# RWKV stage of a one-core decoder step: TensorE's order written out in 137 slots, weight granules fetched two ahead

## The chip, the core and the metric

One core of one Trainium2 chip runs the whole program in one launch. The metric is the device time of that launch in microseconds (us). Five engines work side by side, each through its own queue in order: TensorE (PE, matmuls; its weight loads are shown apart as PEld), VectorE (DVE), ScalarE (ACT), GpSimd (POOL) and SyncE (SP), which here only issues DMAs. They wait for one another by semaphores.

## What is computed

One layer of a recurrent decoder for 320 tokens: a prompt of 256 and 8 samples of 8 new tokens each. A wide projection feeds three branches (HGRN2, RWKV-7, a short gated convolution); they are merged through gates, and an output mix and an MLP follow. The part that the change touches is the RWKV branch and the convolution beside it. Cut to what matters:

```python
rw = proj[..., OFF_RW:OFF_SC]                       # 26 column tiles of 128
xs = rw + (prev - rw) * rw_mu                       # token shift
r, kr, vr, wd, ad, gd = jnp.split(xs, cuts, axis=-1)
decay = exp(-exp(-softplus(-(rw_w0 + tanh(wd) @ rw_w2)) - 0.5)); a = sigmoid(rw_a0 + ad @ rw_a2)
kk = normalized(kr * rw_k_k); k = kr * (1 + (a - 1) * rw_k_a)
# per token: S = S*w + (S @ -kk) (kk*a) + v k ;  o = S r
o_rw, rw_S = _rwkv7_scan(r_, w_, k_, v_, kk, a_, rw_S0)
o_rw = (groupnorm(o_rw) * rw_ln_w + rw_ln_b + bonus) * (sigmoid(gd) @ rw_g2)
y_b = o_rw @ w_pb
u = sc * sh; y_c = (sb * conv3(u)) @ w_pc           # short convolution branch
```

## The kernel before

All activations lie transposed, 128 channels by 320 tokens. A weight matrix is cut into granules of 128 x 1024 floats (512 KB), eight blocks of 128 x 128 for one column tile. `granule` loads one into `raw`, and `split` makes two halves of it on the fly: ACT casts it to `whi_t` (L104) and DVE subtracts to get `wlo_t` (L105), in two pieces of 512 columns. `dense` multiplies 16 blocks (two granules) into one PSUM tile `mm_t`, three matmuls a block (L130 to L132), 48 for a tile. The three buffers each of `raw`, `whi_t` and `wlo_t` are all the lookahead there is.

After a short prologue (norm, the first two column tiles) the RWKV stage works through 8 units of two heads each (`j`). A unit needs three projected tiles (k, r, v, through `shift_mix`), then a chain of small fp32 matmuls with DVE, ACT and POOL work between them:

- `rwkv_front` (L371 to L459): decay and gates, normalised keys, the tiles LYR, BK, X, BT; two reciprocals on DVE (L166, L400).
- `rwkv_solve` (L461 to L549): products of them (L481), a 16 x 16 triangular inverse on DVE in 30 short steps (L512, L514) with a trip through DRAM before and after, and two levels of block inversion on TensorE (L537, L541, L547).
- `rwkv_chunks` (L551 to L679): four chunks of the prompt one behind the other. A chunk is three exchanges: L581/L582, ACT copies Y (L584), L589, DVE copies X (L591), L593/L594, DVE makes the next state (L599 or L601). Behind them in the same function the samples (L614 to L634), the group norm (L642 to L663) and the output (L673 to L679), which is written to `self.B` in SBUF.

`short_conv` projects three more tiles (SC, SH, SB) a unit and leaves its result in `self.Cb` in SBUF. The loop at L360 to L367 writes, for each unit, the solve of the next, the chunks of this one, one convolution, and the front of the one after. The framework's scheduler then orders every engine's queue by priority (the order in which the code was traced) and by its own estimates of time, TensorE's too. Thereafter `merge_split` splits `Cb` into `bh`/`bl`, and HGRN2, the merges with `w_pc`, `w_pb` (from `B`) and `w_pa`, the output mix and the MLP follow; the change leaves their code alone, except that `merge_split` for two of the three sources loads from DRAM.

Of the kernel before, what the change touches and what calls it, by code (L numbers as in the profile page):

```python
# [83 lines left out]
SC_ORDER = ((), (0,), (1,), (2,), (3,), (4,), (5,), (6, 7))  # L84


class K:
# [32 lines left out]
    def dense(self, granules, ah, al):  # L120

        ps = self.mm.tile([128, 512], F32, name="mm_t")
        n = len(granules) * 8
        i = 0
        for g in granules:
            hi, lo = self.granule(g)
            for k in range(8):
                w = slice(k * 128, k * 128 + 128)
                mmul = self.nc.tensor.matmul
                mmul(ps[:, :NT], hi[:, w], ah[:, i, :], start=(i == 0), stop=False)  # L130
                mmul(ps[:, :NT], hi[:, w], al[:, i, :], start=False, stop=False)  # L131
                mmul(ps[:, :NT], lo[:, w], ah[:, i, :], start=False, stop=(i == n - 1))  # L132
                i += 1
        return ps[:, :NT]

# [17 lines left out]
    def proj(self, n):  # L153
# [3 lines left out]
        return self.dense([w[n, 0], w[n, 1]], self.xh, self.xl)  # L157

# [15 lines left out]
    def build(self):  # L174
# [94 lines left out]
        self.merge_split(self.Cb)  # L269
# [5 lines left out]
        for src, i, w in ((self.B, 1, io["w_pb"]), (self.A, 0, io["w_pa"])):  # L275
            self.merge_split(src)
# [14 lines left out]
    def shift_mix(self, wp, n, name, packed):  # L291

        nc = self.nc
        ps = self.proj(n)
# [12 lines left out]
        xs = wp.tile([128, NT], F32, name="xs" + name, bufs=2 if name == "v" else 1)  # L307
# [7 lines left out]
    def rwkv(self, cx):  # L315
# [21 lines left out]
        for nm, cols in (("Nb", 640), ("GB0", 640), ("GB1", 640), ("LX", 256), ("Ms", 256), ("Od", 640)):  # L337
# [21 lines left out]
        st.append(self.rwkv_front(1, wp, w2))
# [9 lines left out]
        nc.sync.dma_start(io["o_shift"], self.shl)  # L369

    def rwkv_front(self, j, wp, w2):  # L371
# [5 lines left out]
        kx = self.shift_mix(w2, RK + j, "k", False)  # L377
        r = self.shift_mix(w2, RR + j, "r", False)
        vx = self.shift_mix(w2, RV + j, "v", True)
# [17 lines left out]
        W = w2.tile([128, NT], F32, name="W")  # L397
        V.tensor_mul(W, Wp, wt[:, 1:])
        Wi = wp.tile([128, NT], F32, name="Wi")
        V.reciprocal(Wi, W)  # L400


        sq = wp.tile([128, NT], F32, name="sq")
# [8 lines left out]
        LYR = w2.tile([128, 5, 4, 64], F32, name="LYR")  # L412
        BK = w2.tile([128, 5, 3, 64], F32, name="BK")
# [12 lines left out]
        S.copy(BK[:, :, 2, :], BK[:, :, 0, :])  # L426
        rk = wp.tile([128, NT], F32, name="rkk")
        V.scalar_tensor_tensor(rk, r, self.par("rk", j), t, ALU.mult, ALU.mult)


        X = w2.tile([128, 5, 2, 64], F32, name="X")
# [12 lines left out]

        bs = self.pa.tile([128, 512], F32, name="pa_t")
# [12 lines left out]

        return W, LYR, BK, X, BT, vx  # L459

    def rwkv_solve(self, j, front, wp):  # L461
        nc, io = self.nc, self.io
        V, G, S, T = nc.vector, nc.gpsimd, nc.scalar, nc.tensor
        W, LYR, BK, X, BT, vx = front
# [5 lines left out]
        Nb = Z["Nb"].rearrange("p (c w) -> p c w", w=128)  # L470
        GB = Z["GB%d" % (j % 2)].rearrange("p (c h w) -> p c h w", h=2, w=64)
        for mk, cc in (("mkp", slice(0, 4)), ("mks", slice(4, 5))):
# [10 lines left out]
            for h, rows in ((0, lo), (1, hi)):  # L483
# [10 lines left out]
                if n == 1:  # L494
                    V.tensor_mul(GB[orow, cc, h, :], p3[orow, :n, cr], mc(orow, cr))

# [6 lines left out]
        nc.sync.dma_start(flat(dN), Z["Nb"])  # L503
# [11 lines left out]
        for c in range(5):  # L515
            nc.sync.dma_start(blocks(dP, c), Pd[8 * c:8 * c + 8])
        nc.sync.dma_start(Z["Pm%d" % (j % 2)], flat(dP))
# [15 lines left out]
        for h in (16, 32):  # L533
            T3 = Z["T%d" % h].rearrange("p (c w) -> p c w", w=128)
            ps = self.pinv.tile([128, 512], F32, name="pi")
            for i in range(4):
                T.transpose(ps[:, blk(i)], Pm[:, i, :], ident)  # L537
            S.copy(Z["Mm"], ps)
            ps = self.pinv.tile([128, 512], F32, name="pi")
# [4 lines left out]
            V.tensor_mul(lev4(Z["T%d" % h], h, 0), ps[:, 0:256].rearrange("p (c n w) -> p c n w", c=4, w=h), mb)  # L544
            ps = self.pinv.tile([128, 512], F32, name="pi")
# [5 lines left out]
    def rwkv_chunks(self, j, front, wp, w2):  # L551
        nc, io = self.nc, self.io
        V, G, S, T = nc.vector, nc.gpsimd, nc.scalar, nc.tensor
        W, LYR, BK, X, BT, vx = front
        Z = self.Z
        ident = self.cst("id")
        lo, hi = slice(0, 64), slice(64, 128)
        GB = Z["GB%d" % (j % 2)].rearrange("p (c h w) -> p c h w", h=2, w=64)
        Pm = Z["Pm%d" % (j % 2)].rearrange("p (c w) -> p c w", w=128)
        s0 = wp.tile([128, 8, 64], F32, name="s0")  # L560
        nc.sync.dma_start(s0, io["s_rw"][j])
        lg = wp.tile([128, 128], F32, name="lg")
        nc.sync.dma_start(lg, io["lg"][:, j * 128:j * 128 + 128])
# [6 lines left out]
        flat = lambda t: t.rearrange("p h w -> p (h w)")  # L570
        alpha = lambda c: flat(LYR[:, c, 0:2, :])
        rho = lambda c: flat(LYR[:, c, 2:4, :])
# [4 lines left out]
        otm = wp.tile([128, 5, 64], F32, name="otm")  # L577
        for c in range(4):
            wc = W[:, c * 64 + 63:c * 64 + 64]
# [5 lines left out]
            if c:  # L585
                for h, rows in heads:
                    G.tensor_scalar_mul(Sw[rows, :], X[rows, c, h, :], wc[rows])
            up = self.py.tile([128, 512], F32, name="py_t")
            T.matmul(up[:, 0:64], Pm[:, c, :], Y, start=True, stop=True)  # L589
            for h, rows in heads:  # L590
                V.tensor_copy(X[rows, c, h, :], up[rows, 0:64])  # L591
            sp = self.py.tile([128, 512], F32, name="py_t")
# [9 lines left out]
        nc.sync.dma_start(io["o_rwp"][j], sn)  # L602
        for h, rows in heads:
            S.copy(otm[rows, 0:4, :], ot4[rows, :, hb(h)])

        LX = Z["LX"].rearrange("p (b a h t) -> p b a h t", a=2, h=2, t=8)
# [12 lines left out]
        yp = self.py.tile([128, 512], F32, name="py_t")  # L621
# [4 lines left out]
        up = self.py.tile([128, 512], F32, name="py_t")  # L626
# [3 lines left out]
        os = self.py.tile([128, 512], F32, name="py_t")  # L630
# [33 lines left out]


        o = wp.tile([128, 5, 64], F32, name="o")
        vx3 = vx.rearrange("p (c w) -> p c w", w=64)
        for cc in (slice(0, 4), slice(4, 5)):
# [5 lines left out]
            for h, rows in heads:  # L674
                V.scalar_tensor_tensor(o[rows, cc], t3[rows, 0:n, hb(h)], self.par("lnw", j)[rows], vx3[rows, cc],
                                       ALU.mult, ALU.add)
        gp = self.pa.tile([128, 512], F32, name="pa_t")
        T.matmul(gp[:, :NT], lg, self.Lg, start=True, stop=True)
        V.tensor_mul(self.B[:, j, :], gp[:, :NT], o.rearrange("p c w -> p (c w)"))  # L679
# [30 lines left out]
    def short_conv(self, j):  # L710
# [4 lines left out]
        scp = self.proj(SC + j)  # L715
        sc = wp.tile([128, NT], F32, name="sc")
        V.tensor_mul(sc, scp, self.rs)
        shp = self.proj(SH + j)
# [14 lines left out]
        sbp = self.proj(SB + j)  # L733
# [466 lines left out]
```

## Time and profile before

| | us |
|---|---|
| median of 3 runs | 2466.48 (2465.77 to 2467.6) |
| the profiled execution's own time | 2465.12 |
| its span in the profile | 2463.3 |
| PE busy, share of the span | 98% |
| PEld busy | 94% |
| DVE, ACT, POOL busy | 61%, 40%, 14% |
| RWKV stage in the trace (end of the prologue's norm to the last write of `B`) | 28.8 to 567.0 |

A row of the windows view gives, for a stretch, its length and then busy time and number of instructions of PE, PEld, DVE, ACT and POOL, the granted clock, the share of DMA time and GB/s. In rows of the lines view stand busy time, mean duration of one in ns, and the idle time of the engine just before it with what ended it. A matmul's end is modelled, so neighbouring rows overlap: the distance between starts is what a matmul costs, not its duration.

### The profile page before, as it was taken

What the parts mean: (1) busy time and instruction counts of PE and PEld (TensorE: products, weight loads), DVE (VectorE), ACT (ScalarE), POOL (GpSimd) and SP (SyncE); (2) the same over time, 40 slices, a digit from 0 to 9 for tenths busy, and PEclk for the clock granted to TensorE, in tenths of its full rate; (3) what the DMA queues carried; (4) which work ended last, traced back from release to release, by engine and by line L of the source; (5) the groups of instructions that cost most, each with busy time, mean ns of one, the idle gap of its engine ahead of it and who ended that gap; (6) DMA issues with size and microseconds to landing.
All of it is one profiled execution on the core that took longest, in us unless ns stands there. A gap on an engine that the chain in (4) does not pass through costs nothing.

```text
span 2463.3 us, 41900 instructions
## 1 busy us (share of the span) xinstructions
PE 2420.1 (98%) x16246; PEld 2325.6 (94%) x16246; DVE 1504.2 (61%) x3097; ACT 996.8 (40%) x1937; POOL 355.8 (14%) x508
## 2 busy tenths in 40 slices
PE   8999999999999999999999999999999999999998
PEld 7888898889999999999999897999999999999996
DVE  6788888866566656655555446754555555555555
ACT  6444444434444344433343435344333333333333
POOL 4333332220000111011111331200000000000003
PEclk9999999999999999999999999999999999999999
DMA  5433333334433333344444654444444444444443
GB/s 192 131 96 122 104 122 107 121 125 142 138 132 138 133 134 128 124 155 152 147 152 146 238 184 165 154 151 148 153 148 152 147 153 149 151 147 153 148 152 129
DMA packets 132278, 354.93 MB, mean 144 GB/s; under 512 B 34928, under 2 KB 43504, under 8 KB 132080
## 3 DMA queue, kind: packets, MB, share of 16 engines
q1 hardware_dynamic: 132080, 352.25, 41.5%
q8 instruction: 129, 2.11, 0.3%
q14 instruction: 69, 0.57, 0.1%
HBM read 337.06 MB, written 15.14 MB: 143 GB/s over the span
## 4 chain that ended last, share of the span: by engine, by line
PE 90%; DVE 6%; POOL 1%; issue 1%; ACT 1%; DMA 0%; SPq 0%; DVEq 0%; ACTq 0%; POOLq 0%
PE mm_t L132 26%; PE mm_t L130 26%; PE mm_t L131 26%; DVE wlo_t L105 1%; PE pi L481 1%; PE pho_t L874 1%; PE pi L541 1%; PE plv_t L834 1%; PE plv_t L835 1%; DVE t L512 0%; PE pi L547 0%; PE py_t L581 0%; DVE Pd L514 0%; DVE rn_y L166 0%; DVE Wi L400 0%
## 5 line engine op out<-in xcount | busy, mean ns | idle before, releaser
L104 ACT CAST whi_t<-raw 128x512 fp32r<-128x512 f32 x1192 | 685.8, 618 | 1161.1 <-PE mm_t L131 728.8
L105 DVE TENSOR_TENSOR wlo_t<-raw,whi_t 128x512 fp32r<-128x512 f32 x1192 | 828.5, 725 | 311.3 <-ACT whi_t L104 300.1
L130 PE MATMUL mm_t<-xh,whi_t 128*128 128x320 f32 x2048 | 643.8, 314 | 1.2 <-DVE Rk L301 1.2
L132 PE MATMUL mm_t<-xh,wlo_t 128*128 128x320 f32 x2048 | 641.8, 314 | 0.4 <-DVE wlo_t L105 0.4
L131 PE MATMUL mm_t<-xl,whi_t 128*128 128x320 f32 x2048 | 640.5, 313 | 0.0
L130 PEld LDWEIGHTS mm_t<-xh,whi_t 128*128 128x128 f32 x2048 | 386.2, 189 | 4.9 <-ACT xsv L448 1.5
L132 PEld LDWEIGHTS mm_t<-xh,wlo_t 128*128 128x128 f32 x2048 | 386.0, 189 | 3.3 <-issue 0.9
L131 PEld LDWEIGHTS mm_t<-xl,whi_t 128*128 128x128 f32 x2048 | 386.0, 188 | 2.0 <-issue 0.2
L130 PE MATMUL mm_t<-hh,whi_t 128*128 128x320 f32 x1232 | 381.4, 310 | 0.0
L131 PE MATMUL mm_t<-hl,whi_t 128*128 128x320 f32 x1232 | 380.7, 309 | 0.0
L132 PE MATMUL mm_t<-hh,wlo_t 128*128 128x320 f32 x1232 | 380.6, 309 | 0.0
L132 PE MATMUL mm_t<-rh,wlo_t 128*128 128x320 f32 x1024 | 316.4, 309 | 0.0
L130 PE MATMUL mm_t<-rh,whi_t 128*128 128x320 f32 x1024 | 316.4, 309 | 0.0
L131 PE MATMUL mm_t<-rl,whi_t 128*128 128x320 f32 x1024 | 316.4, 309 | 0.0
L130 PEld LDWEIGHTS mm_t<-hh,whi_t 128*128 128x128 f32 x1232 | 231.5, 188 | 6.5 <-ACT sqt L1031 4.9
L131 PEld LDWEIGHTS mm_t<-hl,whi_t 128*128 128x128 f32 x1232 | 231.5, 188 | 0.0
L132 PEld LDWEIGHTS mm_t<-hh,wlo_t 128*128 128x128 f32 x1232 | 231.4, 188 | 0.0
L130 PEld LDWEIGHTS mm_t<-rh,whi_t 128*128 128x128 f32 x1024 | 192.2, 188 | 0.0
L131 PEld LDWEIGHTS mm_t<-rl,whi_t 128*128 128x128 f32 x1024 | 192.2, 188 | 0.0
L132 PEld LDWEIGHTS mm_t<-rh,wlo_t 128*128 128x128 f32 x1024 | 192.2, 188 | 0.0
L1102 DVE TENSOR_TENSOR m<-m,mm_t 128x320 f32<-128x320 f32 x112 | 54.6, 488 | 189.5 <-PE mm_t L132 189.5
L1032 POOL TENSOR_TENSOR ssf<-ssf,sqt 128x320 f32<-128x320 f32 x14 | 14.1, 1005 | 841.5 <-issue 809.3
(424 smaller groups left out, 2733.3 us busy)
## 6 DMA issues: line engine op xcount, KB each, us to landing
raw<-w_in SPq DMA_DIRECT2D x256, 512.0 KB
raw<-w_ff SPq DMA_DIRECT2D x256, 512.0 KB
raw<-w_o SPq DMA_DIRECT2D x32, 512.0 KB
hs<-s_hg SPq DMA_DIRECT2D x16, 512.0 KB
raw<-w_pc SPq DMA_DIRECT2D x16, 512.0 KB
raw<-w_pb SPq DMA_DIRECT2D x16, 512.0 KB
raw<-w_pa SPq DMA_DIRECT2D x16, 512.0 KB
o_hgs<-hsn SPq DMA_DIRECT2D x16, 256.0 KB
```

Of the source, the lines that this page charges most:

```text
L104: self.nc.scalar.copy(hi, src)
L105: self.nc.vector.tensor_sub(lo, src, hi)
L130: mmul(ps[:, :NT], hi[:, w], ah[:, i, :], start=(i == 0), stop=False)
L131: mmul(ps[:, :NT], hi[:, w], al[:, i, :], start=False, stop=False)
L132: mmul(ps[:, :NT], lo[:, w], ah[:, i, :], start=False, stop=(i == n - 1))
L481: T.matmul(pp[h][:, i, :], BK[rows, c, h:h + 2, :].rearrange("p a w -> p (a w)"), LYR[rows, c, h:4:2, :], start=True, stop=True)
L541: T.matmul(ps[:, half(i)], Nb[:, i, :], cols(Mm[:, i, :], h, 0), start=True, stop=True)
L834: T.matmul(ps[:, 0:64], KS[:, 0:128], rh[:, 0:hb], start=True, stop=True)
L835: T.matmul(ps[:, 64:128], KS[:, 128:256], rh[:, hb:2 * hb], start=True, stop=True)
L874: T.matmul(op[:, 256:320], s0[:, b, :], QX[:, 64 * b:64 * b + 64], start=(b == 0), stop=False)
L1032: (nc.vector if last else nc.gpsimd).tensor_add(acc, acc, t)
L1102: nc.vector.tensor_add(d, d, ps)
```

## The change

The three functions of a unit become generators that stop at their hand-overs, and so does `dense`, after each block of three matmuls. The group norm and output become `rwkv_tail`, the samples `rwkv_sample`. One loop over 137 slots then writes TensorE's order (`manual_schedule` for PE alone): in slot t, each of the 8 units takes the steps that the tables put there (a unit starts 12 slots after the one before), and then dense blocks are written, 7 a slot in the first 12 slots and 5.5 a slot afterwards. Other engines and the DMA queue are still ordered by the scheduler. Steps of `chunk` and `sample`, the late steps of `solve`, and every fetch of a granule are traced at a priority of 1000 ahead. `fetch` keeps three granules requested: the one in use and two ahead. Convolution tiles are spread: eight of 24 in between the units' tiles, sixteen behind them. `B` and `Cb` no longer lie in SBUF: each 128 x 320 piece is stored to DRAM (`dB`, `dC`) and loaded again, through two buffers `bsrc`, when it is split. Buffers change: `W` and `xsv` 4 (from 2), `LYR`, `X`, `BT`, `GB` 3 (from 2), `Nb` 2 (from 1), `otm` 2 (from 1), `BK` 1 (from 2).

```diff
-SC_ORDER = ((), (0,), (1,), (2,), (3,), (4,), (5,), (6, 7))
+NSLOT = 12
+URGENT = 1000
+FRONT = (-6, -5, 0, 1, 2)
+SOLVE = (1, 2, 9, 15, 16, 17, 18, 19, 20)
+SAMPLE = (20, 21, 22, 23)
+CONV = (3, 0, 1, 1, 1, 1, 1, 0)
+CHUNK = tuple(range(21, 33))
+TAIL = (33, 39, 40)
...
+    def fetch(self):
+        while len(self.ahead) < 3 and self.order:
+            n, h = self.order.pop(0)
+            with self.tc.high_priority(offset=URGENT):
+                self.ahead.append(self.granule(self.io["w_in"][n, h]))
+        return self.ahead.pop(0)
...
-        for j in range(8):
-            if j < 7:
-                self.rwkv_solve(j + 1, st[j + 1], wp)
-            self.rwkv_chunks(j, st[j], wp, w2)
-            for i in SC_ORDER[j]:
-                self.short_conv(i)
-            if j < 6:
-                st.append(self.rwkv_front(j + 2, wp, w2))
+        blocks = (50 - len(self.early)) * 16
+        chains = ((front, FRONT), (sample, SAMPLE), (chunk, CHUNK), (solve, SOLVE), (tail, TAIL))
+        total = 8 * NSLOT + TAIL[-1] + 1
+        with self.tc.manual_schedule(engines={mybir.EngineType.PE}):
+            done = 0
+            for t in range(total):
+                for j in range(8):
+                    for chain, slots in chains:
+                        if t - NSLOT * (j + 1) in slots:
+                            if chain in (chunk, sample) or slots is SOLVE and t - NSLOT * (j + 1) > 9:
+                                with self.tc.high_priority(offset=URGENT):
+                                    next(chain[j], None)
+                            else:
+                                next(chain[j], None)
+                while done < max(7 * min(t + 1, NSLOT), blocks - (blocks - 7 * NSLOT) * (total - 1 - t) // (total - NSLOT)):
+                    next(dense, None)
+                    done += 1
...
-        V.tensor_mul(self.B[:, j, :], gp[:, :NT], o.rearrange("p c w -> p (c w)"))
+        of = o.rearrange("p c w -> p (c w)")
+        V.tensor_mul(of, gp[:, :NT], of)
+        nc.sync.dma_start(self.dB[j], of)
...
-    def merge_split(self, src):
+    def merge_split(self, src, wp):
         for k in range(8):
-            self.split(self.bh[:, k, :], self.bl[:, k, :], src[:, k, :])
+            if wp is None:
+                t = src[:, k, :]
+            else:
+                t = wp.tile([128, NT], F32, name="bsrc")
+                self.nc.sync.dma_start(t, src[k])
+            self.split(self.bh[:, k, :], self.bl[:, k, :], t)
```

TensorE before, two exchanges of one chunk in the middle of the stage (unit 2; L581, L589 and L593 are the chunk's matmuls, the others dense):

```order
L581 MATMUL py_t<-X,LYR 128x128
L582 MATMUL po_t<-X,LYR 128x128
L131 MATMUL mm_t<-xl,whi_t 128x320
L132 MATMUL mm_t<-xh,wlo_t 128x320
L589 MATMUL py_t<-Y,Pm_388 128x64
L130 MATMUL mm_t<-xh,whi_t 128x320
L131 MATMUL mm_t<-xl,whi_t 128x320
L132 MATMUL mm_t<-xh,wlo_t 128x320
L130 MATMUL mm_t<-xh,whi_t 128x320
L131 MATMUL mm_t<-xl,whi_t 128x320
L593 MATMUL py_t<-X,BT 128x128
```

TensorE of the change, an exchange of the same kind (L685 is the old L589, L690 the old L593, L740 and L745 belong to the samples of the same unit, L142 to L144 are the dense matmuls):

```order
L740 MATMUL pa_t<-Y_2430,Pm_400 128x64
L685 MATMUL py_t<-Y,Pm_400 128x64
L142 MATMUL mm_t<-xh,whi_t 128x320
L143 MATMUL mm_t<-xl,whi_t 128x320
L144 MATMUL mm_t<-xh,wlo_t 128x320
...
L745 MATMUL pa_t<-c,Ms 128x128
L746 MATMUL pa_t<-X,GB_408 128x128
L690 MATMUL py_t<-X,BT 128x128
```

Before, two to five dense matmuls stand between a chunk's matmul and the one that needs its result back; now 15 (as here) or 18 do, in every slot.

DVE before, from the copies of X (L591) to the state (L601) of a first chunk, unit 1:

```order
L591 COPY X<-py_t 64x64 x2
L619 COPY Ms<-pa_t 64x4x4x8 x2
L601 TENSOR_SCALAR X<-py_t,W 64x64 x2
L300 TENSOR_TENSOR Rk<-mm_t,rs 128x256
```

DVE of the change at the same place (L687 is the old L591, L698 the old L601, L116 the split of a granule):

```order
L687 COPY X<-py_t 64x64
L602 TENSOR_TENSOR t_2140<-Nd,Pd 40x3x13
L116 TENSOR_TENSOR wlo_t<-raw,whi_t 128x512 x2
...
L772 TENSOR_TENSOR otm<-otm,gs 128x320
L861 SCALAR_TENSOR_TENSOR cv<-u,p,cv 128x336
L776 TENSOR_REDUCE gv<-sq_2475 128x5
L698 TENSOR_SCALAR X<-py_t,W 64x64 x2
```

Twenty-five instructions now stand between the copies and the state at this place, where two stood; a similar stretch stands in unit 0, and in the later units a few instructions do.

SP before, where the merge with `w_pb` begins, issues weights alone:

```order
L112 DMA raw<-w_pb 128x1024
L112 DMA raw<-w_in 128x1024 x2
L112 DMA raw<-w_pb 128x1024
L112 DMA raw<-w_in 128x1024 x2
L112 DMA raw<-w_pb 128x1024
```

SP of the change at the same place (`bsrc<-dB` are the pieces of the RWKV output; the first two of the eight were loaded long before):

```order
L123 DMA raw<-w_pb 128x1024
L123 DMA raw<-w_in 128x1024 x2
L1095 DMA bsrc<-dB_348 128x320
L1095 DMA bsrc<-dB_349 128x320
L123 DMA raw<-w_pb 128x1024
L1095 DMA bsrc<-dB_350 128x320
L1095 DMA bsrc<-dB_351 128x320
L123 DMA raw<-w_in 128x1024
L1095 DMA bsrc<-dB_352 128x320
L1095 DMA bsrc<-dB_353 128x320
```

Six loads, each pair of which needs the two buffers that the splits of the pair before give back, now stand in this queue among the weights.

More of the change, by code (lines that the diff above doesn't have):

```diff
@@ L125, in dense @@
         for g in granules:
-            hi, lo = self.granule(g)
+            hi, lo = self.fetch() if g is None else self.granule(g)
             for k in range(8):
@@ L133, in dense, with run @@
                 i += 1
+                if i < n:
+                    yield
         return ps[:, :NT]
+    @staticmethod
+    def run(steps):
+        while True:
+            try:
+                next(steps)
+            except StopIteration as e:
+                return e.value
+    def dense(self, granules, ah, al):
+        return self.run(self.dense_steps(granules, ah, al))
     def dense_wide(self, tiles, ah, al, psp, wpool):
@@ new lines, in rwkv @@
+        dense = self.rwkv_dense(w2)
+        front = [self.rwkv_front(j, wp, w2) for j in range(8)]
+        solve = [self.rwkv_solve(j, wp) for j in range(8)]
+        chunk = [self.rwkv_chunks(j, wp, w2) for j in range(8)]
+        sample = [self.rwkv_sample(j, wp) for j in range(8)]
+        tail = [self.rwkv_tail(j, wp) for j in range(8)]
+        blocks = (50 - len(self.early)) * 16
+        chains = ((front, FRONT), (sample, SAMPLE), (chunk, CHUNK), (solve, SOLVE), (tail, TAIL))
+        total = 8 * NSLOT + TAIL[-1] + 1
@@ new lines, in rwkv @@
+        with self.tc.manual_schedule(engines={mybir.EngineType.PE}):
[12 more added lines that the diff above has]
+                    done += 1
+            self.run(dense)
+            for c in front + solve + chunk + sample + tail:
+                assert next(c, 0) == 0
@@ L368, in rwkv, with rwkv_dense @@
         nc.sync.dma_start(io["o_cv"], self.cvo)
         nc.sync.dma_start(io["o_shift"], self.shl)
+    def rwkv_dense(self, w2):
+        S = self.nc.scalar
+        tiles, conv = [], [(c, j) for j in range(8) for c in (SC, SH, SB)]
+        for j in range(8):
+            tiles += [(RK, j), (RR, j), (RV, j)] + ([(RG, 0)] if j == 1 else [])
+            for _ in range(CONV[j]):
+                tiles.append(conv.pop(0))
+        tiles = [(RWA, 0)] + tiles + conv
+        self.order = [(n + j, h) for n, j in tiles if n + j not in self.early for h in range(2)]
+        self.ahead = []
+        done = {}
+        for n, j in tiles:
+            if n in (SC, SH, SB):
+                c = done.setdefault(j, self.short_conv(j))
+                for end in c:
+                    yield
+                    if end:
+                        break
+                continue
+            name = {RK: "k", RR: "r", RV: "v", RWA: "k", RG: "k"}[n]
+            quick = n + j in self.early
+            xs = yield from self.shift_mix(w2, n + j, name)
+            if n == RWA:
+                S.activation(self.L[0:64, :], xs[0:64, :], AF.Tanh)
+                S.copy(self.L[64:128, :], xs[64:128, :])
+            elif n == RG:
+                S.activation(self.Lg, xs, AF.Sigmoid)
+            else:
+                self.st[j][name] = xs
+            if not quick:
+                yield
```

158 lines of the change are left out of this document (101 added, 57 removed).

## The prediction

> **What bounds the kernel now.** The views in the order in which I read them: the windows view, to find where TensorE loses time; the timeline at one hand-over, to see what a loss looks like; the lines view of DVE, for what its queue holds. Windows first: the RWKV stage, then a piece of its beginning, four units of its middle, and three stretches after it.
>
> ```profile
> 28.80:567.00 538.20, 515.02 (x3467) 467.78 (x3466) 435.03 (x1149) 236.21 (x499) 168.30 (x334) 0.99 0.35 116
> 28.80:160.00 131.20, 120.30 (x767) 108.30 (x766) 103.45 (x267) 61.05 (x120) 48.34 (x109) 0.96 0.37 121
> 224.00:289.00 65.00, 62.99 (x432) 56.89 (x432) 53.35 (x147) 28.61 (x63) 23.49 (x42) 1.00 0.33 110
> 289.00:354.00 65.00, 63.03 (x434) 57.57 (x433) 52.16 (x140) 28.85 (x61) 19.73 (x38) 1.00 0.36 118
> 354.00:419.00 65.00, 63.25 (x434) 58.03 (x434) 53.75 (x142) 29.16 (x62) 20.26 (x40) 1.00 0.36 117
> 419.00:484.00 65.00, 63.23 (x435) 58.12 (x434) 53.70 (x143) 29.36 (x62) 18.14 (x33) 1.00 0.37 119
> 616.00:677.00 61.00, 61.00 (x422) 59.34 (x421) 36.20 (x82) 24.34 (x48) 5.34 (x6) 1.00 0.41 138
> 1170.00:1231.00 61.00, 61.00 (x418) 61.00 (x418) 35.13 (x55) 24.55 (x48) 7.70 (x6) 1.00 0.42 147
> ```
>
> From 616 us on PE has no idle time, and in dense work (1170 to 1231) PEld has none either: nothing is to be had there. In the RWKV stage PE is idle for 538.2 - 515.0 = 23.2 us, nearly half of it (10.9) before 160 us, and PEld for 538.2 - 467.8 = 70.4 us. What has to be known is how much of that is waiting. One hand-over in the middle, PE's rows and then ACT's:
>
> ```profile
> 301.45 0.46 PE L581 MATMUL py_t<-X,LYR 128*128 128x128 f32 x2
> 301.75 0.39 PE L582 MATMUL po_t<-X,LYR 128*128 128x128 f32 x2
> 301.89 0.39 PE L132 MATMUL mm_t<-xh,wlo_t 128*128 128x320 f32 x1
> 302.12 0.31 PE L130 MATMUL mm_t<-xh,whi_t 128*128 128x320 f32 x1
> 302.79 0.43 PE L589 MATMUL py_t<-Y,Pm 128*128 128x64 f32 x2 [0.36 <-ACT Y L584]
> 301.70 0.58 ACT L730 ACTIVATE cv<-u,p 128x336 f32<-128x336 f32 x1 [1.93 <-POOL u L726]
> 302.30 0.44 ACT L584 COPY Y<-py_t 64x64 f32<-64x64 f32 x2
> ```
>
> Two dense matmuls are all the cover between L581 and L589; ACT is busy with L730 until 302.28, copies Y after it, and PE stands. A dense matmul costs 61.00 / 418 = 0.146 us from the 1170 row, but 0.67 us pass between the starts at 302.12 and 302.79: 0.52 is lost, and the row shows 0.36. So PE's 23.2 us are too little, because the modelled end of a matmul covers the first part of a wait. PEld's 70.4 are too much, because a small fp32 matmul keeps the weight path less busy than a dense one. I take the middle, **46.8 us**, and keep both ends. A page bears on this choice: the Trainium skill, Perfetto Trace Analysis, section Identifying the Most-Contended Engine, says to judge TensorE by the busy share of its weight loads and not by that of its matmuls. By the page alone the loss would be 70.4; the 1170 row agrees in dense work, and the hand-over lies between the two.
>
> **The change, part by part.** First the PE floor of the stage. It holds 48 tiles of 48 dense matmuls:
>
> ```profile
> L130 PE MATMUL mm_t<-xh,whi_t 128*128 128x320 f32 x766 | 246.2, 321 | 1.2 <-DVE Rk L301 1.2
> ```
>
> 766 of the 768 of this line are in the trace; 3 x 768 x 0.146 = 336.4 us. The other 201.8 us are small matmuls and waits; less 46.8 this leaves 155.0, or 19.4 us of small matmuls a unit. The change removes and adds none of either. It only puts 15 or 18 dense matmuls, 2.2 or 2.6 us, behind every step, where two to five stood; the exchange above takes about a microsecond when nothing is in its way (0.46 for L581, 0.44 for the copies, and the hops). **Term 1: -46.8 us** (from -23.2 to -70.4) if every hand-over is covered.
>
> Second, what stays late. PE's time falls and DVE's does not, so DVE is what to look at:
>
> ```profile
> L105 DVE TENSOR_TENSOR wlo_t<-raw,whi_t 128x512 fp32r<-128x512 f32 x191 | 128.9, 693 | 11.4 <-ACT whi_t L104 9.0 <-ACT Y L584 1.1
> L166 DVE RECIPROCAL rn_y<-rn_t 128x320 f32<-128x320 f32 x8 | 17.1, 2136 | 0.0
> L400 DVE RECIPROCAL Wi<-W 128x320 f32<-128x320 f32 x8 | 16.9, 2114 | 0.0
> L731 DVE SCALAR_TENSOR_TENSOR cv<-u,p,cv 128x336 f32<-128x336 f32 x8 | 4.5, 567 | 2.6 <-ACT cv L730 2.5
> L717 DVE TENSOR_TENSOR sc<-mm_t,rs 128x320 f32<-128x320 f32 x8 | 3.9, 490 | 1.2 <-PE mm_t L132 1.0
> ```
>
> In the four middle units DVE is busy 53.2 us of 65, with six tiles (12 granules) each. In the change a unit comes every 12 slots. 768 dense blocks less the 84 of the first 12 slots, over 125 slots, are 5.47 a slot; 12 slots hold 65.7 blocks, or 8.2 granules, 65.7 x 3 x 0.146 = 28.8 us of PE, and with 19.4 a period of **48.2 us**. DVE has 3.8 granules fewer to split, each two pieces of 0.693 (5.3 us), and two of three convolution tiles fewer (2.6 us a convolution: 0.49 three times, about 0.57 twice; two thirds are 1.7): **46.2 us** busy in 48.2. Before, it had 11.8 us idle in a unit; now 2.0. All five chains overlap from slot 33 (the tail of unit 0) to about 98 (the last front), 65 / 12 = 5.4 periods. A copy of a chunk that comes just behind a reciprocal starts up to 2.1 us late, against 2.2 us of cover less the 1 us of the exchange: 0.9 late, twice a unit. I take 2 us a period, 11 us (from 0, if the rows' overlap on DVE leaves more room than busy time says, to 53, the rival below). Then the one bad place in DVE's order: in unit 1 (and much the same in unit 0) 25 instructions stand between the copies of X and the state of the first chunk. At the stage's mean of 435.03 / 1149 = 0.379 us they are 9.5 us; the state is wanted two slots (8.0 us) after L685, an exchange of 1 us included: 2.5 late, 5 for the two units (0 to 10). **Term 2: +16 us.**
>
> Third, the output through DRAM. Before, the eight splits of `B` run under the gate projection; a store and the load behind it show what a trip costs:
>
> ```profile
> L104 ACT CAST bh<-B x8: 446/455/457, 1044.5 to 1047.0; 128x320 fp32r<-128x320 f32 x8
> L105 DVE TENSOR_TENSOR bl<-B,bh x8: 474/476/477, 1045.5 to 1048.7; 128x320 fp32r<-128x320 f32 x8
> ...
> 233.42 0.33 SPq L503 DMA_DIRECT2D dN<-Nb  x1
> 235.57 1.76 SPq L507 DMA_DIRECT2D Nd<-dN  x5
> ```
>
> The splits can start at 1044.5, and the gate projection gives 48 x 0.146 = 7.0 us, so block k of `bh` is wanted at 1051.5 + 0.44 k. In the change three pairs must be loaded after the first has been split: each round is a DMA of 2.15 us (a store of twice the size, 233.42 to 235.57) and two casts and a subtraction, 1.4 us. The last pair is ready at about 1044.5 + 1.4 + 3 x 3.55 = 1056.5 and wanted at 1054.1: 2.4 late, and SP has 512 KB loads between the pairs. **Term 3: +3 us** (0 to 8). The same detour for `Cb` is free: its casts stood at 569.8 and their first use was at 608.2, 38 us later:
>
> ```profile
> L130 PE MATMUL mm_t<-bh,whi_t x384: 307/309/394, 608.2 to 1382.6; 128*128 128x320 f32 x192
> L104 ACT CAST bh<-Cb x8: 453/456/460, 569.8 to 572.3; 128x320 fp32r<-128x320 f32 x8
> ```
>
> That cover ends when HGRN2's first projections no longer fill PE. The 16 stores and 16 loads of 160 KB run on DMA engines that were busy for 35% of the stage: nothing. On SP each store waits for the instruction of DVE or POOL that makes its piece, and weights stand in the queue behind it; but the granules asked for ahead cover that, as a granule is used in 48.2 / 8.2 = 5.9 us. The two-ahead fetch alone is worth little: the L130 row has 1.2 us of idle time, none of it for a weight.
>
> **Sum**, made against the profiled execution (2465.12 us, 1.4 below the median of 2466.48): -46.8 + 16 + 3 = -27.8, so 2437.3 there, and **2438 us** beside the median.
>
> **The rivals.**
>
> *Slower: DVE keeps its idle time.* If its queue, now fixed against a TensorE order that leaves it no choice, still waits 11.8 us a unit, a period is 46.2 + 11.8 = 58.0 and not 48.2: 9.8 x 5.4 = 53. Then -46.8 + 53 + 3 = +9, 2476. It decides from a period of 48.2 + (46.8 - 3) / 5.4 = 56.3 us. For it: 96% is more than any engine but PE reaches here. Against: much of the 11.8 is DVE waiting for PE, which the longer cover takes away.
>
> *No change: the rows on DVE no longer overlap.* Neighbouring DVE rows overlap now:
>
> ```profile
> 302.31 0.57 DVE L731 SCALAR_TENSOR_TENSOR cv<-u,p,cv 128x336 f32<-128x336 f32 x1 [1.01 <-ACT cv L730]
> 302.80 0.68 DVE L105 TENSOR_TENSOR wlo_t<-raw,whi_t 128x512 fp32r<-128x512 f32 x1
> ```
>
> The second starts 0.08 us before the first ends. If the new order, with more dependent neighbours, took that from each of some 125 instructions a unit, DVE would need 46.2 + 10 = 56.2 us: 8.0 x 5.4 = 43, and -46.8 + 43 + 3 gives 2466. The Trainium skill, VectorE: DVE Perf Modes, section The DRAIN you can't avoid, says that the next operation doesn't start before the pipe is empty, which speaks against this change; the same page names operations that start earlier, and these two rows do.
>
> *A small gain.* Only the 23.2 us are waiting. The small matmuls then are 178.6 us, a period 51.1, and DVE has room: no loss in the periods, 5 + 3 elsewhere: 2451.
>
> *A large gain.* All 70.4 us go. Small matmuls are 131.4, a period is 45.2, DVE binds at 46.2: 1.0 x 5.4 more than the 16 + 3: -46, 2420.
>
> **How the numbers follow.** Forecast 0.56, large gain 0.09, small gain 0.16, no change 0.08, slower 0.11. About 0.2% (5 us) is what a measurement of this kernel can tell from no change; so faster 0.81, same 0.08, slower 0.11. The range goes from below the large gain, 2412, to just over the no-change case, 2468; it leaves out the slower rival and a tail below.
>
> **What would show it.** Right: the stage ends at about 536 us (567 - 47 + 16) and not 567; PE idle in it well under 23 us, PEld idle near 25; L685 and L690 hardly wait in the middle units; DVE's busy share there is above 90%; a wait of a few us for `bh` or `bl` at the first w_pb tile, and none at the first w_pc tile. A wait of PE for L698 of units 0 and 1 shows the 5 us, waits spread over all units the 11. It is wrong if the middle units come every 52 us or more, if a whole granule is late at PE (the waits of L142 and L144), or if the DMA queue holds weights behind stores that wait for DVE.

## The result, and the profile after

The changed kernel takes **2497.18 us** (median; 2495.77 to 2499.67), the kernel before on the same chip 2466.12: a ratio of 1.0121, 95% interval 1.0106 to 1.0136. It is 31 us slower where 28 us faster was forecast. The profiled execution took 2497.74 us, with a span of 2496.0 against 2463.3: 32.7 us more.

The windows view of the changed kernel: length of the stretch, then busy us and instructions of PE, PEld, DVE, ACT and POOL, the granted clock, DMA share, GB/s. The first row is the whole RWKV stage, then its beginning and the four stretches of 65 us that the prediction showed for the kernel before.

```profile
28.80:594.70 565.90, 500.24 (x3469) 479.98 (x3468) 445.83 (x1149) 237.10 (x501) 164.23 (x337) 0.94 0.36 114
28.80:160.00 131.20, 112.50 (x745) 107.20 (x744) 96.42 (x222) 59.51 (x104) 44.85 (x105) 0.91 0.39 122
224.00:289.00 65.00, 58.70 (x409) 55.78 (x409) 57.32 (x155) 29.24 (x68) 23.75 (x47) 0.95 0.35 110
289.00:354.00 65.00, 55.05 (x393) 51.87 (x393) 56.70 (x159) 27.74 (x62) 19.52 (x39) 0.93 0.33 101
354.00:419.00 65.00, 56.49 (x378) 53.81 (x378) 52.26 (x145) 25.28 (x58) 18.16 (x36) 0.91 0.33 99
419.00:484.00 65.00, 56.66 (x404) 54.11 (x403) 54.51 (x146) 26.17 (x58) 16.93 (x32) 0.95 0.34 107
```

The stage ends at 594.7 and not at 567.0. PE is idle in it for 65.7 us (23.2 before), and two things that no row of before had stand here: PE idle for 6 to 10 us in every 65, and a granted clock of 0.91 to 0.95 (1.00 before). The first matmul with `bh`, where HGRN2's merges begin, starts at 635.9 and not 608.2: 27.6 of the 32.7 us have been lost by then. 4.3 more are lost at the first tile with `w_pb`, 0.8 behind it.

Whom PE waits for in the stage, by the waits view (sum of us, times, longest us). L142 to L144 are the dense matmuls (L130 to L132 before), L569 the products at the start of a solve (L481 before):

```profile
PE pi L569 <- DVE GB L581: 17.2, 9, 3.4
PE mm_t L142 <- DVE Rv L341: 12.7, 2, 7.8
PE mm_t L142 <- DVE sh L850: 11.2, 2, 7.2
PE mm_t L142 <- DVE Pd L604: 9.7, 1, 9.7
PE mm_t L142 <- DVE sb L866: 5.1, 2, 4.7
PE pa_t L735 <- DVE Ms L730: 2.8, 2, 1.4
PE mm_t L142 <- ACT whi_t L115: 1.8, 1, 1.8
...
PE py_t L676 <- DVE X L698: 1.6, 1, 1.6
...
PE py_t L685 <- ACT Y L679: 0.2, 1, 0.2
```

The chunks' hand-overs L685 and L690 stand in it with 0.2 us in all, and a granule was late once at most, for 1.8 us (the emptying of `sc` ended only 0.1 us before that matmul). The row with `Pd` is an emptying of a tile, too: its matmul began at 119.15, and DVE's last piece of that tile's `Rv` (L341) ended at 119.01. What is late is DVE, with two jobs that the prediction did not name: emptying a finished dense tile out of PSUM (Rv, sh and sb are what is made from `mm_t`), of which there are two buffers, and emptying the two buffers `pi` of a solve's first step. One of these waits, PE's rows first:

```profile
163.92 0.31 PE L143 MATMUL mm_t<-xl,whi_t 128*128 128x320 f32 x1
164.07 0.31 PE L144 MATMUL mm_t<-xh,wlo_t 128*128 128x320 f32 x1
172.17 0.64 PE L142 MATMUL mm_t<-xh,whi_t 128*128 128x320 f32 x1 [7.79 <-DVE Rv L341]
172.60 0.47 PE L143 MATMUL mm_t<-xl,whi_t 128*128 128x320 f32 x1
172.87 0.47 PE L144 MATMUL mm_t<-xh,wlo_t 128*128 128x320 f32 x1
```

and DVE's rows of the same time:

```profile
154.59 2.13 DVE L481 RECIPROCAL Wi<-W 128x320 f32<-128x320 f32 x1
156.65 1.21 DVE L116 TENSOR_TENSOR wlo_t<-raw,whi_t 128x512 fp32r<-128x512 f32 x2
...
161.75 0.54 DVE L512 SCALAR_TENSOR_TENSOR rkk<-xsr,p,tk 128x320 f32<-128x320 f32 x1
162.22 0.19 DVE L602 TENSOR_TENSOR t<-Nd,Pd 40x48 f32<-40x48 f32 x1
162.33 2.13 DVE L207 RECIPROCAL rn_y<-rn_t 128x320 f32<-128x320 f32 x1
164.40 1.21 DVE L116 TENSOR_TENSOR wlo_t<-raw,whi_t 128x512 fp32r<-128x512 f32 x2
...
169.19 0.55 DVE L493 SCALAR_TENSOR_TENSOR rn_y<-xsk,p,rn_y 128x320 f32<-128x320 f32 x1
169.86 0.43 DVE L340 TENSOR_TENSOR Rv<-mm_t,rs 128x256 f32<-128x256 f32 x1
...
171.50 0.48 DVE L508 SCALAR_TENSOR_TENSOR BK<-rn_y,a 128x320 f32<-128x320 f32 x1
171.90 0.21 DVE L341 TENSOR_TENSOR Rv<-mm_t,rs 128x64 f32<-128x64 f32 x1
```

The tile of v had its last matmul at about 154 (48 dense matmuls before the one at 164.07). DVE empties it between 169.86 and 172.11, and no row of DVE between 154.59 and 172 has any idle time in front of it: two reciprocals, the splits, the next front and the recursion (L602/L604) stand first in its queue. PE has written the other buffer full by 164.4 and stands for 7.8 us. Then its dense matmuls start 0.27 us apart (172.60, 172.87), not 0.146.

To see where all of it went I compared every distance between the starts of neighbouring matmuls of the stage, from 28.8 to the first matmul with `bh`, with the lower quartile that the same pair of kinds has over all runs. What is over by 0.35 us or more is called a long wait, other excess at half clock "half", the rest "short":

| us | as undisturbed | long waits | of them L142 and L569 | half | short | sum |
|---|---|---|---|---|---|---|
| before | 493.1 | 25.0 | 1.4 | 3.4 | 57.8 | 579.3 |
| after | 493.0 | 66.2 | 58.0 | 22.4 | 25.5 | 607.1 |

How the parts divide depends on which matmuls count as one kind. With kinds told apart by shape alone, and dense ones from the others, the six columns read 485.4, 30.5, 1.9, 3.2, 60.1 and 579.2 before, 486.2, 73.0, 61.9, 22.5, 25.2 and 606.9 after. The parts move by up to 8 us, and no reading below turns on it. The 41.9 and 20.0 us of long waits in the expectations of e1 and e2 are of this second count.

The change did what the prediction took as its gain, and paid for it with late DVE and a slower clock.

### The profile page after: what moved, and what is told of

Its sections match the earlier page's. It is cut to its first block, busy times and chain, and to the rows that moved or that the text cites. A ratio compares the mean times of both kernels' runs of the same rounds, so it can differ in the third digit from the quotient of the medians.

```text
span 2496.0 us, 41979 instructions
## 1 busy us (share of the span) xinstructions
PE 2406.8 (96%) x16246; PEld 2338.4 (94%) x16246; DVE 1517.0 (61%) x3097; ACT 997.7 (40%) x1939; POOL 350.6 (14%) x510
## 4 chain that ended last, share of the span: by engine, by line
PE 80%; DVE 2%; DMA 1%; POOL 0%; ACT 0%; issue 0%; SPq 0%; DVEq 0%; ACTq 0%; POOLq 0%
PE mm_t L142 24%; PE mm_t L144 24%; PE mm_t L143 24%; PE pho_t L1007 1%; PE plv_t L967 1%; DVE wlo_t L116 1%; PE plv_t L968 1%; PE wide_t L1078 0%; PE wide_t L1079 0%; PE wide_t L823 0%; DMA bsrc<-dB 0%; DVE m L1265 0%; DMA raw<-w_o 0%; POOL ssb L1159 0%; PE plv_t L970 0%
## 5 line engine op out<-in xcount | busy, mean ns | idle before, releaser
L116 DVE TENSOR_TENSOR wlo_t<-raw,whi_t 128x512 fp32r<-128x512 f32 x1192 | 835.7, 733 | 324.3 <-ACT whi_t L115 315.3
L142 PE MATMUL mm_t<-xh,whi_t 128*128 128x320 f32 x2048 | 655.8, 320 | 40.5 <-DVE Rv L341 12.7
L144 PE MATMUL mm_t<-xh,wlo_t 128*128 128x320 f32 x2048 | 642.4, 314 | 0.0
L142 PEld LDWEIGHTS mm_t<-xh,whi_t 128*128 128x128 f32 x2048 | 392.5, 192 | 49.3 <-ACT BK L509 17.5
L143 PEld LDWEIGHTS mm_t<-xl,whi_t 128*128 128x128 f32 x2048 | 392.8, 192 | 1.1
L144 PEld LDWEIGHTS mm_t<-xh,wlo_t 128*128 128x128 f32 x2048 | 392.1, 191 | 0.3
L142 PE MATMUL mm_t<-hh,whi_t 128*128 128x320 f32 x1232 | 381.6, 310 | 0.0
L144 PE MATMUL mm_t<-hh,wlo_t 128*128 128x320 f32 x1232 | 380.7, 309 | 0.0
L144 PE MATMUL mm_t<-rh,wlo_t 128*128 128x320 f32 x1024 | 316.4, 309 | 0.0
L142 PE MATMUL mm_t<-rh,whi_t 128*128 128x320 f32 x1024 | 316.4, 309 | 0.0
L142 PEld LDWEIGHTS mm_t<-hh,whi_t 128*128 128x128 f32 x1232 | 231.5, 188 | 6.3 <-ACT sqt L1169 4.9
L144 PEld LDWEIGHTS mm_t<-hh,wlo_t 128*128 128x128 f32 x1232 | 231.4, 188 | 0.0
L142 PEld LDWEIGHTS mm_t<-rh,whi_t 128*128 128x128 f32 x1024 | 192.2, 188 | 0.0
L144 PEld LDWEIGHTS mm_t<-rh,wlo_t 128*128 128x128 f32 x1024 | 192.2, 188 | 0.0
```

The costliest lines, as they stand in the source:

```text
L116: self.nc.vector.tensor_sub(lo, src, hi)
```

## The experiments

All medians of experiments stand beside runs of the kernel before on the same chip (2467.6 to 2468.2). Three columns are the parts of the table above. "Prio" is the edit of e1 and e2 together.

| run | median us | ratio to before, 95% | long | half | short |
|---|---|---|---|---|---|
| changed kernel | 2497.2 | 1.0106 to 1.0136 | 66.2 | 22.4 | 25.5 |
| e1, evacuations first | 2486.9 | 1.0063 to 1.0093 | 56.9 | 20.3 | 24.4 |
| e2, prio | 2481.7 | 1.0041 to 1.0071 | 55.1 | 18.8 | 25.6 |
| e3, no priority | 2506.9 | 1.0143 to 1.0173 | 74.5 | 26.8 | 24.7 |
| e4, PE's order free | 2497.4 | 1.0098 to 1.0132 | 44.1 | 13.5 | 51.4 |
| e5, prio + dense to the middle | 2455.3 | 0.9936 to 0.9966 | 33.8 | 9.2 | 25.1 |
| e6, prio + less on DVE | 2459.2 | 0.9950 to 0.9979 | 39.3 | 13.1 | 25.8 |
| e7, e5 + e6 + more buffers | 2443.2 | 0.9886 to 0.9915 | 22.6 | 16.9 | 24.2 |
| e8, before + trip through DRAM | 2472.1 | 1.0009 to 1.0028 | | | |
| e9, changed + dense to the middle | 2481.5 | 1.0037 to 1.0070 | 53.6 | 18.9 | 26.0 |
| e10, changed + less on DVE | 2488.6 | 1.0062 to 1.0096 | 55.6 | 22.2 | 24.4 |
| e11, e7, solve a slot later | 2457.5 | 0.9942 to 0.9972 | 34.6 | 15.6 | 25.4 |
| e12, e11, 7.0 blocks a slot | 2455.0 | 0.9935 to 0.9964 | 34.2 | 13.7 | 26.7 |
| e13, prio + front 3 slots earlier | 2468.9 | 0.9996 to 1.0014 | 38.7 | 16.1 | 29.2 |
| e14, e7, front 3 slots earlier | 2448.5 | 0.9908 to 0.9942 | 31.3 | 10.6 | 26.1 |
| e15, prio + dense within a unit | 2472.4 | 1.0014 to 1.0033 | 47.9 | 17.8 | 24.9 |

### e1, e2: what PE waits for goes first

```diff
-        nc.vector.tensor_mul(R[:, 1:257], ps[:, :NP], self.rs[:, :NP])
+        with self.tc.high_priority(offset=URGENT):
+            nc.vector.tensor_mul(R[:, 1:257], ps[:, :NP], self.rs[:, :NP])
...
-                            if chain in (chunk, sample) or slots is SOLVE and t - NSLOT * (j + 1) > 9:
+                            if chain in (chunk, sample, solve):
```

> The five instructions with which DVE empties a finished dense tile (L340, L341, L846, L850, L866) get the same priority in the scheduler as the granules have; nothing else is changed. Theory A (a finished tile waits in DVE's fixed queue behind work that is not wanted yet; TensorE has two PSUM buffers for dense tiles and an order that it can't leave, so it stands, and its clock drops afterwards): the long waits of L142, 41.9 us in the stage, and about two thirds of the 19.4 us that the half clock costs go away, so 2497 - 42 - 13 = 2442, between 2430 and 2460; the waits of L569 stay near 20 us. Theory B (DVE has no room in a unit of 56 us, whatever stands first in its queue): the waits move to L569, L685 and L690, and the time stays within 8 us of 2497.

> As the first run, and the first steps of the solve (L569 to L581, the recursion L602 to L604, L677 behind them) get the priority too, which only its last steps had. Theory A: the 20.0 us of long waits of L569 go as well, with the rest of the half clock: 2497 - 42 - 20 - 19 = 2416, between 2405 and 2440. Theory B: within 8 us of 2497, the waits move to L142, L685 and L690.

e1 gained 10 us, e2 15; theory A had wanted 55 and 81, theory B under 8. The waits of L142 went to nothing, as A said. The waits view of e1 from 100 to 470 us (line numbers one to three higher than in the changed kernel) shows what came, as B said:

```profile
PE pi L570 <- DVE GB L582: 15.8, 8, 3.5
PE pa_t L522 <- DVE xsv L350: 13.1, 3, 7.5
PE pi L570 <- DVE BK L509: 4.9, 2, 2.9
PE pa_t L747 <- DVE X L743: 4.0, 4, 1.4
```

The tile of v is now emptied at once, but the instruction of DVE that makes `xsv` from it is as late as the emptying was, and the transposes at L522 wait for that. So neither theory holds alone: DVE's order says where the wait falls, and something else that there is one.

### e3, e4: neither the priorities nor PE's fixed order is the harm

```diff
-URGENT = 1000
+URGENT = 0
```

> The priority offset is 0 in place of 1000 everywhere; order of slots, two granules ahead and all buffers stay. Theory A: what has priority is not what PE waits for, so without it the evacuations come in the order of the program; the waits of L142 shrink and those of L685, L690 and L634 grow: about even, 2480 to 2510. A third theory C (the priority itself does the harm, because splits of granules two ahead stand before evacuations): the waits of L142 go and none comes, 2445 to 2465. Theory B: 2490 to 2505.

```diff
-        with self.tc.manual_schedule(engines={mybir.EngineType.PE}):
+        with ExitStack():
```

> The order of TensorE is no longer fixed by the slots: the code is written in the same order, but the scheduler places TensorE's instructions like those of the other engines. Theory A: part of the harm is that TensorE can't run around a late tile, so the long waits get shorter, 2455 to 2480, at the price of short hand-overs as before. Theory B: DVE's load is the same, so the time stays within 8 us of 2497.

Without priority it is 10 us slower; theory C falls. Waits for `Ms` of the samples took the place of most of those of L142; the first row of the waits view of e3:

```profile
PE pa_t L735 <- DVE Ms L730: 32.5, 6, 8.1
```

With PE's order left to the scheduler the time is the same to 0.3 us, B's number and not A's (2455 to 2480), though what A said of the waits came: long waits and half clock fall by 31 us, but the short hand-overs come back to 51.4, near the 57.8 of before, and the undisturbed part is 5 us longer. This prices the fixed order by itself: it saves 26 us of short waits and costs about as much, because PE stands where it could run around a late tile.

### e5, e6, e7: more for PE beside DVE's work, or less for DVE

```diff
-CONV = (3, 0, 1, 1, 1, 1, 1, 0)
+CONV = (3, 1, 2, 2, 2, 2, 2, 0)
...
-                while done < max(7 * min(t + 1, NSLOT), blocks - (blocks - 7 * NSLOT) * (total - 1 - t) // (total - NSLOT)):
+                last = int(84 + 6.6 * 86)
+                want = int(84 + 6.6 * (t + 1 - NSLOT)) if t < 98 else last + (blocks - last) * (t - 97) // (total - 98)
+                while done < (7 * (t + 1) if t < NSLOT else want):
```

> The run with evacuations and solve first (2481.7), and beside that another share of dense work: 6.6 blocks a slot from slot 12 to 97 in place of 5.47, and 3.0 a slot after it. Theory B (DVE is busy 47 us in a unit and gets no further than 86 to 88% of the time, so a unit takes 54 us whatever TensorE has to do): a unit then holds 13.6 blocks more, 5.9 us of TensorE for 3.0 us of DVE, so about 2.9 us of waiting a unit go, 20 us in seven units, and the thin slots at the end give back 0.3 us each, 12: 2474, between 2460 and 2481. Theory O (each wait is an accident of the order, whatever DVE's load): the waits of the middle stay, and the end costs 12: 2494.

```diff
-        V.tensor_scalar(t, a, self.par("ka", j), self.omka[:, j:j + 1], ALU.mult, ALU.add)
+        S.activation(t, a, AF.Identity, bias=self.omka[:, j:j + 1], scale=self.par("ka", j))
...
-                V.tensor_copy(X[rows, c, h, :], up[rows, 0:64])
+                S.copy(X[rows, c, h, :], up[rows, 0:64])
```

> The run with evacuations and solve first (2481.7), and beside that some of DVE's work is done by ACT, which is busy under half of the time: the copies of X (L687, L742 of the changed kernel, ten a unit, 0.21 us each), the two copies of Ms (0.29 each) and the scaling of a (L504, 0.43), together 3.1 us a unit. Theory B: a unit gets shorter by as much, 3.1 x 7 = 22 us, and the half clock by some: 2458, between 2450 and 2468. Theory O: within 8 us of 2482.

```diff
-                t = wp.tile([128, NT], F32, name="bsrc")
+                t = wp.tile([128, NT], F32, name="bsrc", bufs=8)
```

> Both of the last two, and eight buffers in place of two for the pieces that come back from DRAM, so that the loads for w_pb needn't wait for the splits. Theory B: 2482 - 8 - 22 - 4 = 2448, between 2436 and 2462. Theory O: 2490.

Theory B, and not O, has the direction three times, and the size twice. e5 gained 26 us against e2 where 8 were expected, and its 2455.3 lies below B's range of 2460 to 2481: the thin slots at the end, priced at 12 us, cost nothing that shows (short waits 25.1 against 25.6), and the other 6 us stay unexplained. e6 gained 22.5, as expected. e7 gained 38.5 and at 2443.2 us is faster than both kernels, 1.0% below the kernel before. The stretch from 100 to 470 us of the changed kernel and of e2, e5, e6 and e7, in this order, in the windows view:

```profile
100.00:470.00 370.00, 314.50 (x2176) 298.84 (x2175) 306.54 (x824) 157.59 (x339) 109.53 (x216) 0.92 0.34 103
```

```profile
100.00:470.00 370.00, 323.72 (x2259) 305.45 (x2259) 317.54 (x848) 158.75 (x346) 119.13 (x223) 0.94 0.37 107
```

```profile
100.00:470.00 370.00, 342.87 (x2461) 328.26 (x2460) 330.14 (x852) 169.62 (x365) 120.40 (x229) 0.98 0.42 121
```

```profile
100.00:470.00 370.00, 334.35 (x2371) 318.05 (x2371) 310.18 (x803) 183.91 (x446) 119.38 (x224) 0.95 0.41 113
```

```profile
100.00:470.00 370.00, 352.76 (x2500) 338.52 (x2498) 319.19 (x790) 191.43 (x447) 125.99 (x236) 0.96 0.43 121
```

In equal time PE gets through 2176 matmuls, then 2259, 2461, 2371 and 2500, while DVE is busy for 83, 86, 89, 84 and 86%: more work for PE, or less for DVE, is what lets PE go on. Part of the counts of e5 and e7 is the dense work that was moved into this stretch.

### e8: the trip through DRAM by itself

> The kernel before, with nothing changed but that the outputs of the tails and convolutions go through DRAM, as in the changed kernel. From the trace of the changed kernel, which loses 4.3 us in the first tile with w_pb against the kernel before and nothing at the first with w_pc: +4, 2470.5, between 2468 and 2475. The rival (stores that wait for DVE hold the weights behind them on the queue, and this is part of the loss in the RWKV stage): +10 or more, 2478.

The kernel before with `B` and `Cb` stored to and loaded from DRAM takes 4.3 us more than the kernel before (interval 2.2 to 6.9), the +4 of the expectation. Where they lie fits less well: of the 6.1 us by which its trace is longer, 2.6 are lost at the first tile with `w_pb`, 1.3 ahead of it and 2.2 behind. The rival, stores that hold up the weights and cost 10 us or more, falls for this kernel.

### e9, e10: the same edits without the priorities

> The changed kernel as it is (2497), with 6.6 blocks of dense work a slot from slot 12 to 97 alone; priorities as in the change. Theory B (the load of DVE in a unit makes the waits, the order only says where they fall): as much as behind the other priorities, 26 us: 2471, between 2460 and 2480. Theory A (the evacuations that wait in DVE's queue are a cause by themselves, and have to go first): more dense tiles only bring more late evacuations, within 8 us of 2497.

> The changed kernel as it is (2497), with the copies of X and Ms and the scaling of a on ACT alone. Theory B: 22 us less, as behind the other priorities: 2475, between 2466 and 2483. Theory A: within 8 us of 2497.

Both lie between the theories: dense work moved to the middle gives 16 us and not 26, less on DVE 9 and not 22. The waits view of e10, from 100 to 470 us, shows why so little:

```profile
PE mm_t L142 <- DVE Rv L341: 22.9, 3, 10.8
PE pi L569 <- DVE GB L581: 19.4, 11, 3.9
```

A late evacuation stays late: over the whole stage the waits of L142 come to 32.0 us, of 40.5 in the changed kernel. Priority alone is worth 15 us and dense work to the middle 16, both together 42 and not 31: each is worth more where the other has been done.

### e11, e12: a slot more for the solve's first step

```diff
-SOLVE = (1, 2, 9, 15, 16, 17, 18, 19, 20)
+SOLVE = (1, 3, 10, 15, 16, 17, 18, 19, 20)
```

> The run with both (2443.2), and the second step of a solve comes in slot 3 and not in slot 2 of its unit, the third in slot 10 and not 9, so that DVE has two slots in place of one to empty the two PSUM buffers of the first step. Theory A for this place (a step that needs six instructions of DVE is given one slot of 4 us): the 19.3 us of long waits of this matmul go, and half of the 16.9 us at half clock: 2443 - 19 - 8 = 2416, between 2408 and 2430. Theory B: DVE is as busy as before, the waits move on: 2436 to 2446.

> As the last, with 7.0 blocks a slot from slot 12 to 97 and 2.1 after it. Theory B: a unit holds 4.8 blocks more, 2.1 us of TensorE against 1.1 us of DVE, so 1.0 x 7 = 7 us less waiting, against 39 slots with 0.9 block less cover at 0.1 to 0.3 us, 4 to 12 back: within 6 us of the last run. Where DVE no longer bounds a unit: up to 12 slower than the last run.

A miss, and no theory had it: 14 us slower than e7. The first row of the waits view of e7, then two of e11:

```profile
PE pi L572 <- DVE GB L584: 10.5, 9, 2.5
```

```profile
PE pi L572 <- ACT Mm L633: 11.9, 7, 2.9
PE pi L572 <- DVE BK L511: 9.6, 3, 4.8
```

Slot 3 of a unit is slot 15 of the one before it, and there another solve uses the same two PSUM buffers: 11.9 us of waits for the emptying of `Mm` by ACT stand where 10.5 us of waits for DVE stood, and PE waits besides for the chunks' states, and once, for 4.2 us, for the solve's inverse on its way through DRAM. e12 came within 6 us of e11, as expected; more dense work than 6.6 blocks a slot brings nothing there that the measurement can tell.

### e13, e14, e15: is DVE's idle time in one place?

It was still open why DVE, busy for 83% of the changed kernel's middle, could not use the rest. The changed kernel's unit from 329 to 385.5 us in quarters:

```profile
329.00:343.00 14.00, 11.89 (x86) 11.46 (x85) 13.70 (x27) 6.86 (x21) 4.91 (x5) 1.00 0.53 151
343.00:357.00 14.00, 10.59 (x73) 9.52 (x74) 12.46 (x38) 3.59 (x8) 3.01 (x7) 0.82 0.29 99
357.00:371.00 14.00, 14.00 (x99) 13.80 (x99) 8.88 (x27) 3.31 (x8) 3.70 (x7) 0.93 0.26 74
371.00:385.50 14.50, 13.07 (x95) 12.11 (x94) 13.88 (x43) 10.00 (x18) 6.40 (x13) 1.00 0.29 84
```

DVE is busy for 98, 89, 63 and 96% of the quarters; PE loses its time in the first, second and last, and nothing in the third, where DVE has room. Theory U (full here, half idle there) against theory M (only the mean load counts, and the number of hops, the hand-overs from engine to engine):

```diff
-FRONT = (-6, -5, 0, 1, 2)
+FRONT = (-9, -5, 0, 1, 2)
```

> The run with evacuations and solve first (2481.7), and the first step of a front (the decay, with the scan, a product and the first reciprocal of 2.1 us, 3.2 us of DVE in all) comes three slots earlier, in slot -9 and not -6, where DVE is busy for 55 to 90% of the time in the trace and not for 97% or more; nothing is added or taken away. Theory U (DVE is full in one part of a unit and waits in another): 3 us a unit less waiting, as when 3.1 us were moved to ACT: 2460, between 2450 and 2470. Theory M (only the mean load and the hops count): within 6 us of 2482.

> The run with both (2443.2), with the same step three slots earlier. Theory U: its long waits are 22 us and its half clock 17 us, half of them may go: 2425, between 2415 and 2437. Theory M: within 6 us of 2443.

```diff
-                while done < max(7 * min(t + 1, NSLOT), blocks - (blocks - 7 * NSLOT) * (total - 1 - t) // (total - NSLOT)):
+                even = blocks - (blocks - 7 * NSLOT) * (total - 1 - t) // (total - NSLOT)
+                more = (7, 8, 6, 4, 2, 0, 1, 2, 3, 4, 5, 6)[t % NSLOT] if 30 <= t < 98 else 0
+                while done < max(7 * min(t + 1, NSLOT), even + more):
```

> The run with evacuations and solve first (2481.7), with one more dense block in each of the eight slots from 6 to 1 of a unit (DVE full) and two fewer in each of slots 2 to 5 (DVE half idle); every unit holds as many as before. Theory U: each of the eight slots gets 0.44 us of cover for 0.2 us of DVE, 2 us a unit: 2468, between 2460 and 2477. Theory M: within 6 us of 2482; where the slots with less cover begin to wait, up to 10 slower.

e13 and e15 come out within U's bounds: 13 and 9 us less than e2 with the same work in every unit, only in other slots. The gains are smaller than U's middle values (22 and 14). On top of e7 the early front brings nothing (2448.5, M's number): most of what PE waited for is gone there, and the early step meets new waits of its own, 8.8 us in two at its first matmul (L468), for which the profile names no releaser. So the uneven load is shown as a cause in the order of 10 us; how the rest divides between hops and load stays open.

## Why the prediction was wrong

**Term 1, -46.8 us: right.** The short waits fell by 32.3 us (57.8 to 25.5), and the long waits at places other than L142 and L569 from 23.6 to 8.2: 47.7 together, 52.4 by the second count. The middle between PE's idle time (23.2) and PEld's (70.4) came out right, though it was a choice between two bounds that no row had measured. L685 and L690 hardly wait any more, as said, and e4 shows that it is the fixed order that does it. The Trainium skill, Perfetto Trace Analysis, section Identifying the Most-Contended Engine, would have had 70.4 as the loss. The measured 47.7 disagrees: in the changed kernel's stage, where most of the short waits are gone, PEld is still idle for 20.2 us more than PE (85.9 against 65.7), so up to about 20 of the 70.4 are not lateness.

**Term 2, +16 us: the step that failed.** Late DVE cost 56.6 us more at L142 and L569 (58.0 less 1.4), and the clock that follows such waits 19.0 (22.4 less 3.4): 75.6 in place of 16 (79.3 by the second count). The load was right: DVE is busy for 306.54 of 370 us, and a unit's first chunk starts every 56.1 us between 217.5 and 441.9, so 46.5 us a unit where 46.2 were forecast; the share is 83%, though, and not above 90. Wrong was what was made of it: "46.2 us busy in 48.2", then 2 us a period. A mean over twelve slots was taken as if DVE could serve any slot of them. In the slots of the front and the solve it had no gap for 18 us on end, and each step there has one slot of 4 us; two buffers for dense tiles carry PE over one late tile, not two. So the period was 56.1 us and not 48.2: 7.9 us, over the 5.4 periods of the sum 43 in place of 11. The rest came where the sum had next to nothing: by the second count 37.8 of the 84.4 us of these waits and of half clock fall ahead of 217.5 us (slot 33), before all five chains overlap. The bad place that I looked for in DVE's order, the states of units 0 and 1, cost nothing in the waits view, not 5 (its one wait for a state, the 1.6 us of L676, came at 283.5 in unit 2); the prediction looked through DVE's queue for the chunks alone, and not for the other thing that PE needs from it, empty PSUM.

**The clock** was in no term and no rival. Before, it stood at half for 10.2 us of the stage; after, ten times and 68.3 us in all.

**Term 3, +3 us: right.** PE waits for `bh` at `w_pb`; from the changed kernel's timeline:

```profile
1077.05 0.89 ACT L115 CAST bh<-bsrc 128x320 fp32r<-128x320 f32 x2 [3.05 <-DMA bsrc<-dB]
1085.34 0.42 PE L142 MATMUL mm_t<-bh,whi_t 128*128 128x320 f32 x1 [1.97 <-ACT bh L115]
1086.62 0.47 PE L142 MATMUL mm_t<-bh,whi_t 128*128 128x320 f32 x1
```

The first tile with `w_pb`, from its first matmul to that of the next tile with `bh`, takes 21.1 us before, 23.7 in e8 and 25.4 here: 4.3 more, 2.6 of them as in e8. The row at 1086.62 is already at half clock, which lasts 3.4 us here (1086.0 to 1089.4) and does not come at this place in e8. `w_pc` lost nothing, as forecast. -47.7 + 75.6 + 4.3 = 32.2, and 0.5 of small change, make the 32.7 us of the span.

**The rivals.** The slower one, "DVE keeps its idle time", was what happened in the middle units. That its 53 us for the waits stand so near to 56.6, and its 2476 with the 19 of the clock to the measured time, is luck in part: all of its 53 were to fall in 5.4 periods, which cost 43 with the clock included, and it had nothing ahead of them. I gave it 0.11, on the ground that much of the idle time was DVE waiting for PE, which longer cover takes away. It did not go: a unit of 56.1 us with 46.5 busy leaves 9.6 idle, of 11.8 before. "No change", by rows that no longer overlap, falls: busy time a unit is as forecast. Of the signs that I named, the period of 52 us or more was the right one; waits of L142 came, but for a PSUM buffer and not for a granule.

## What to carry to other kernels

When a fixed order is to hide an engine's work behind another's, hold that engine's load against the cover slot by slot, not as a mean over a period, and go through everything that the waiting engine needs from it, the emptying of its PSUM buffers included. An instruction that frees a buffer belongs in the same priority as the chain that is being hurried; but priority alone mostly moves the wait (15 us gained of the 81 that theory A had wanted), and what pays is to lay the plentiful work (here dense matmuls) beside the engine that is full and to take work off it. A slot table has to be read modulo its period: what is moved out of one chain's way lands in another's.

## What the runs showed of the hardware

A wait of TensorE costs more than its length. In sixteen traces (all but that of e8), of the waits of 2.5 us or more between two matmuls of the stage that began at full clock, 77 of 78 had the clock fall to half during the wait or within 4 us of its end; of the 24 of 2.5 to 3.4 us among them 23; of those of 2 to 2.5 us 16 of 25, of 1.5 to 2 us 17 of 41 (some of these had another wait beside them). The waits are the idle times that the profile shows. In the changed kernel the clock stays at half for 3.4, 6.8 or 10.2 us; a dense matmul then starts every 0.267 us (median of some 130 in the stage) against 0.146, and ten such falls cost 22.4 us beside the waits: 2.2 us each. The Trainium skill, TensorE: Matmul & The Clock Gate, section HAM oscillation — how this bites in real kernels, gives gaps of over about 3.4 us as the bound; by these runs it is lower, 2.5 us sufficed nearly always.
